# Value sets moved ahead of forget sets, first forget loads and the pairs' operations given rank, in a hybrid HGRN2 and attention block

## The chip, the core and the metric

The kernel runs on one core of a Trainium2 chip. The metric is the time of one execution on the device in microseconds, as the median of several runs; lower is better. The core has five engines that take instructions in order, each from its own queue: TensorE (PE) multiplies matrices, VectorE (DVE) and ScalarE (ACT) work on elements, GpSimd (POOL) here mostly issues transfers, and SyncE (SP) issues the loads of the weights. Engines wait for each other through semaphores.

## The reference

One transformer block over 256 tokens and 256 context tokens of width 2048. All projections come from one matrix, `xn @ w_in`; two branches, a sliding-window attention and a bidirectional gated linear recurrence (HGRN2) of 16 heads of 128, are gated, projected and merged. The part around the change:

```python
xn = rmsnorm(h, norm_gain[l]) * (1.0 + scale) + shift      # cn likewise from ctx
aq, ak, av, ag, hq, hff, hfb, hi, hg, ma, mb = split_columns(xn @ w_in[l])
...
g_f, k_f = hgrn_forget(hff, lb_f_all[l])     # log f and 1-f, f = lb + (1-lb)*sigmoid(z)
g_b, k_b = hgrn_forget(hfb, lb_b_all[l])     # the same for the context: cg_*, ck_*
v_h = to_heads(hi); q_h = to_heads(jax.nn.silu(hq))
s_f = hgrn2_final_state(ck_f, cv_h, cg_f)    # start states from the context
s_b = hgrn2_final_state(flip_t(ck_b), flip_t(cv_h), flip_t(cg_b))
o, _, _ = hgrn2_bidir(q_h, v_h, k_f, g_f, k_b, g_b, s_f, s_b)
hg_branch = hgrn_readout(o, hgrn_norm_gain[l], hg)
```

All of it is float32. The kernel gets that precision from a reduced format by splitting each operand into a high and a low part and multiplying high by high, low by high and high by low.

## The kernel before

**Weights.** A weight tile of 512 KB is loaded by SP's queue into one of four buffers (`raw`). ScalarE copies its high part (`wh`, L76 in general chunks, L605 in the dense phase), VectorE subtracts to get the low part (`wl`, L77, L606); each has three buffers. A chunk of products then runs on TensorE: L91, L92 and L94, or L145 and L148 for the query projections.

**Stages.** After normalisation comes the *dense phase*. It makes the first value projection, one output gate, then 13 column sets and 3 value sets. A column set, `quad_col(d, n)`, computes the forgets F of direction d for two heads with seven sums of products instead of eight (L630 and L633, the operand T or `raw` combined on VectorE, L586; results joined in L623, L624 and L649). Partial sums of a set stand in a tile `s15`, which uses the buffer of the tag `F1` (there is one). F itself uses one of the two buffers of the tag `F0`, and POOL stores it to a DRAM tensor (L655). A value set, `quad_tok`, does the same for values (L702, L704, L707; joined by VectorE in L664); its two result tiles `vo` use both `F0` buffers and POOL stores them (L712).

**Pair stage.** Then eight pairs of heads are worked one after another. `load_forgets(n)` loads F of both directions for pair n back from DRAM into an `F0` and an `F1` buffer (L1089, on POOL's queue, F1 first in the code) and `ctx_decay` runs over the context half: two scans per direction on VectorE (L759 forward, L763 backward; the trace calls them TENSOR_TENSOR_SCAN, the lists of instructions below SCALAR_TENSOR_TENSOR) and one product per direction (L764, into the context half of F). Then the four query chunks are projected and `pair` does the rest: transposes of the context half (`tw`, L904), `grow` (L882, L883, L887, L888) with copies on ScalarE (L814, L817), score blocks `al` (L841), their masking (L856 on VectorE, L853 on ScalarE), `kt` (L947), the state (L967), the outputs `ob` (L979 to L981) and the readout (L991). L783, L788 to L792 prepare its operands, L156 joins the halves of the query projections. `pair` is a generator: it gives up control between its parts, and `weave` puts projections for other parts of the block between them, as many columns as the pair asked for, so that TensorE has work while VectorE and ScalarE do the pair's. Every three such steps a gate chunk of `w_ada` is loaded and summed on VectorE (L196).

**What sets the order.** In both stages TensorE's order is the order of the code. The other engines are ordered ahead of time by a list scheduler: of the instructions that are ready by its own model, the one with the highest priority is next, which is by default the one written first. `tc.high_priority(n)` raises what is written inside it by n. Chunks have `PRIO` (100000), the joining of the sets 2 * `PRIO`, the pairs and `ctx_decay` nothing. Once put in order, an engine's instructions are run in that order, whatever arrives first. A buffer is handed on when the last reader of its former tile is done.

Of the kernel before, what the change touches and what calls it, by code (L numbers as in the profile page):

```python
# [21 lines left out]
PRIO = 100000  # L22

C_Q, C_K, C_V, C_G = 0, 2048, 2560, 3072
C_HQ, C_FF, C_FB, C_HI, C_HG = 5120, 7168, 9216, 11264, 13312
# [13 lines left out]
def block_kernel(ctx: ExitStack, tc: tile.TileContext, x, c, cx, c_ctx, w_ada, b_ada, norm_gain, w_in,  # L39
# [59 lines left out]
    def proj_tok_g(w, col0, src, toks):  # L99


        banks = [bank() for _ in toks]
        for k0 in range(0, KT, 2):
            h, lo = wchunk(w, k0 * P, 2, col0, 512)
            mm_high_first([(banks[i], src(k0 + j, t), (h[:, j, :], lo[:, j, :]), k0 + j == 0, k0 + j == KT - 1)
                           for j in range(2) for i, t in enumerate(toks)])
            yield len(toks) * 6 * 512
        return banks
# [9 lines left out]
    def proj_tok(*a):  # L118
        return result(proj_tok_g(*a))
# [100 lines left out]
    v_dr = [[dram.tile([P, 1024], F32, name=f"v{g}_{t}") for t in range(2)] for g in range(4)]  # L220
# [285 lines left out]
    def run(g):  # L506
        for _ in g:
            pass

    def output_gate(g):  # L510
        bg = yield from proj_tok_g(w_in, C_HG + 512 * g, x_st, range(2))
        for t in range(2):
            sg = base.tile([P, 512], F32, tag="sm", name="sgg", bufs=3)
            act.activation(sg, bg[t], AF.Sigmoid)
            dve.tensor_tensor(sg, bg[t], sg, op=ALU.mult)
            nc.gpsimd.dma_start(hg_dr[g][:, t * 512: (t + 1) * 512], sg)
# [17 lines left out]
    with pl("sp", reuse_waits="tile") as sp:  # L534
# [179 lines left out]
        with tc.manual_schedule(engines={mybir.EngineType.PE}):  # L714
            bv0 = proj_tok(w_in, C_HI, x_st, range(4))
            for g in range(2):
                token_sums(g)
            for t in range(2):
                vo = fp.tile([P, 2, 512], F32, tag="F0", name="vo", bufs=2)
                with tc.high_priority(2 * PRIO):  # L720
                    act.activation(vo[:, 0, :], bv0[t], AF.Copy)
                    dve.tensor_copy(vo[:, 1, :], bv0[2 + t])
                nc.gpsimd.dma_start(v_dr[0][t], vo.rearrange("p a c -> p (a c)"))
            run(output_gate(0))
            for n in range(1, 8):
                for d in range(2):
                    if (d, n) != (0, 1):
                        quad_col(d, 2 * n)
            for g in range(1, 4):
                quad_tok(C_HI + 512 * g, v_dr[g])  # L730

    biases = {}

# [16 lines left out]
    def ctx_decay(F):  # L750


        rev = lambda a: bass.AP(a.tensor, a.offset + T - 2, [list(a.ap[0]), [-1, T - 1]])
        for d in range(2):
            e = base.tile([P, 512], F32, tag="sm", name="e", bufs=3).rearrange("p (h t) -> p h t", h=2)
            for i in range(2):
                if d == 0:
                    pool.memset(e[:, i, T - 1: T], 1.0)
                    dve.tensor_tensor_scan(rev(e[:, i, 0: T - 1]), rev(F[0][:, i, T + 1: 512]), zeros[:, : T - 1], 1.0,  # L759
                                           ALU.mult, ALU.add)  # L760
                else:
                    pool.memset(e[:, i, 0:1], 1.0)
                    dve.tensor_tensor_scan(e[:, i, 1:T], F[1][:, i, T: 511], zeros[:, : T - 1], 1.0, ALU.mult, ALU.add)  # L763
            dve.scalar_tensor_tensor(F[d][:, :, T:], F[d][:, :, T:], -1.0, e, op0=ALU.add, op1=ALU.mult)  # L764
# [248 lines left out]
    def weave(g, filler):  # L1013

        ahead = 0
        for want in g:
            ahead -= want * STEP
            while ahead < 0:
                got = next(filler, None)
                if got is None:  # L1020
                    break
                ahead += got
        run(filler)
# [62 lines left out]
    def load_forgets(n):  # L1086
        F = [fp.tile([P, 2, 512], F32, tag=f"F{d}", name=f"F{d}", bufs=2 - d) for d in range(2)]
        for d in (1, 0):
            nc.gpsimd.dma_start(F[d].rearrange("p i t -> p (i t)"), F_dr[d][n])  # L1089
        ctx_decay(F)  # L1090
        return F
# [48 lines left out]
    with tc.manual_schedule(engines={mybir.EngineType.PE}):  # L1140
        accT = fp.tile([P, 2, 512], F32, tag="acc", name="acc")
        gate, count = gates(), [0]
        grps = [[None] * 3 for _ in range(4)]
        res = [load_forgets(0), None]
        res[1] = result(proj_col_x_g(w_in, C_HQ))
        for n in range(8):
            if n % 2 == 0:
                load_values(n // 2, grps[n // 2])
                load_gate(n // 2, grps[n // 2])
            nxt = [None] * 2  # L1150
            weave(pair(n // 2, n % 2, grps[n // 2], *res), with_gates(inputs(n, nxt)))
            res = nxt
        for f in done:
            f()
# [334 lines left out]
```

## Time and profile before

| | |
|---|---|
| runs | 1617.05, 1620.55, 1621.6 us; median 1620.55 |
| the profiled execution | 1618.51 us, of which the span is 1616.7 us |
| granted TensorE clock, mean over the span | 0.993 |
| TensorE busy | 1581.5 us (98%) |
| VectorE busy | 1153.2 us (71%) |
| ScalarE busy | 863.5 us (53%) |
| moved by DMA | 312.76 MB, mean 193 GB/s |

A row of the page's groups reads: line, engine, operation, output from input, count, then total busy time and mean nanoseconds of one, then the engine's idle time before such instructions and what ended most of it. A row of the waits view names the engine and line that waited, what it waited for, and then total microseconds, times, and the longest. In a timeline row stand start, duration and instruction, and in brackets how long the engine had been idle before it and what released it. In a row of windows stand the stretch and its length, busy time and count for PE, PEld, DVE, ACT and POOL, then the granted clock, the DMA engines' busy share and GB/s.

### The profile page before, as it was taken

The page shows a single profiled execution, that of the slowest core. Times are in us where ns is not written, and L with a number is a line of the kernel's source. Part 1 is how long each engine was busy: PE and PEld are TensorE (multiplying, and loading weights), DVE is VectorE, ACT ScalarE, POOL GpSimd, SP SyncE. Part 2 cuts the span into 40 slices and gives each one's busy share as a digit, 9 for nine tenths or more (in the row PEclk, how much of TensorE's full clock was granted, in tenths as well). Part 3 has the DMA queues.
Part 4 walks back from the last instruction along what each step waited for, and adds up shares of the span by engine and source line. Part 5 has one row for each costly group of instructions (what it writes and reads, how often), then busy time and mean ns, then how long its engine had stood idle before and what let it go on. Part 6 is the DMA issues. An engine that isn't in the chain of part 4 may idle for free. (4 is left out here: it accounts for less than half of the span.)

```text
span 1616.7 us, 26661 instructions
## 1 busy us (share of the span) xinstructions
PE 1581.5 (98%) x10522; PEld 1337.2 (83%) x10522; DVE 1153.2 (71%) x1703; ACT 863.5 (53%) x1337; POOL 84.0 (5%) x183
## 2 busy tenths in 40 slices
PE   7999999999999989999999999999999999999997
PEld 4567888888899978888888888878888888888887
DVE  4449688888877767885887887556567767756664
ACT  4334456656543345664666566434457677744442
POOL 2000000000000010111111010000000000000000
PEclk9999999999999999999999999999999999999999
DMA  9994444444444466664777776567554445467662
GB/s 365 386 371 168 156 131 130 134 142 142 134 141 131 131 241 209 196 222 144 233 242 231 225 237 204 163 213 244 181 183 144 144 138 166 159 230 242 198 208 80
DMA packets 230013, 312.76 MB, mean 193 GB/s; under 512 B 10080, under 2 KB 145664, under 8 KB 228992
## 3 DMA queue, kind: packets, MB, share of 16 engines
q1 hardware_dynamic: 216800, 266.85, 50.5%
q0 software_dynamic: 12368, 43.11, 7.7%
q8 instruction: 82, 1.34, 0.3%
q10 hardware_dynamic: 720, 1.11, 0.2%
q14 instruction: 43, 0.35, 0.1%
HBM read 290.05 MB, written 20.98 MB: 192 GB/s over the span
## 5 line engine op out<-in xcount | busy, mean ns | idle before, releaser
L77 DVE TENSOR_TENSOR wl<-raw,wh 128x1024 fp32r<-128x1024 f32 x308 | 374.6, 1221 | 184.0 <-ACT wh L76 166.6
L76 ACT ACTIVATE wh<-raw 128x1024 fp32r<-128x1024 f32 x308 | 324.8, 1059 | 311.9 <-PE pj L92 189.2
L91 PE MATMUL pj<-wh,xHL 128*128 128x512 f32 (+1 forms) x832 | 326.1, 393 | 2.4 <-DVE hsum L156 1.7
L92 PE MATMUL pj<-wh,xHL 128*128 128x512 f32 (+1 forms) x832 | 320.7, 387 | 0.0
L94 PE MATMUL pj<-wl,xHL 128*128 128x512 f32 (+1 forms) x832 | 215.3, 386 | 0.0
L91 PEld LDWEIGHTS pj<-wh,xHL 128*128 128x128 f32 x832 | 157.0, 189 | 35.2 <-DVE hsum L156 2.6
L92 PEld LDWEIGHTS pj<-wh,xHL 128*128 128x128 f32 x832 | 157.1, 189 | 29.7
L94 PEld LDWEIGHTS pj<-wl,xHL 128*128 128x128 f32 x832 | 154.5, 188 | 32.1 <-DVE wl L77 0.5
L145 PE MATMUL pj<-xHL,wh 128*128 128x512 f32 x512 | 130.8, 397 | 0.0
L605 ACT ACTIVATE wh<-raw 128x1024 fp32r<-128x1024 f32 x76 | 80.4, 1058 | 74.3 <-PE pj L630 22.1
L606 DVE TENSOR_TENSOR wl<-raw,wh 128x1024 fp32r<-128x1024 f32 x76 | 92.8, 1221 | 33.0 <-ACT wh L605 32.9
L145 PEld LDWEIGHTS pj<-xHL,wh 128*128 128x128 f32 x512 | 92.6, 188 | 17.3
L91 PE MATMUL pj<-wh,bH 128*128 128x512 f32 x256 | 101.7, 398 | 3.4 <-ACT wh L76 2.7
L605 ACT ACTIVATE wh<-T 128x1024 fp32r<-128x1024 f32 x57 | 60.5, 1061 | 80.4 <-PE pm L630 19.4
L92 PE MATMUL pj<-wh,bL 128*128 128x512 f32 x256 | 100.8, 395 | 0.1
L606 DVE TENSOR_TENSOR wl<-T,wh 128x1024 fp32r<-128x1024 f32 x57 | 69.6, 1220 | 19.8 <-ACT wh L605 19.6
L148 PEld LDWEIGHTS pj<-xHL,wl 128*128 128x128 f32 x512 | 69.8, 190 | 5.2
L94 PE MATMUL pj<-wl,bH 128*128 128x512 f32 x256 | 71.4, 395 | 0.1
L148 PE MATMUL pj<-xHL,wl 128*128 128x256 f32 x512 | 71.3, 282 | 0.0
L196 DVE SCALAR_TENSOR_TENSOR acc<-raw,cg,acc 128x512 f32<-128x512 f32 x60 | 44.9, 748 | 31.6 <-DMA raw<-in_w_ada_dram 31.1
L887 DVE TENSOR_TENSOR A<-A,X 128x512 f32<-128x512 f32 x96 | 61.9, 685 | 4.5 <-ACT F L814 2.8
L91 PEld LDWEIGHTS pj<-wh,bH 128*128 128x128 f32 x256 | 48.8, 191 | 14.8 <-ACT wh L76 3.6
(356 smaller groups left out, 2763.2 us busy)
## 6 DMA issues: line engine op xcount, KB each, us to landing
raw<-in_w_in_dram SPq DMA_DIRECT2D x300, 512.0 KB, 3.8
raw<-in_w_ada_dram SPq DMA_DIRECT2D x96, 512.0 KB, 7.8
raw<-in_w_o_hgrn_dram SPq DMA_DIRECT2D x32, 512.0 KB, 4.7
raw<-in_w_o_attn_dram SPq DMA_DIRECT2D x32, 512.0 KB, 3.9
F<-F POOLq DMA_DIRECT2D x29, 512.0 KB, 4.8
raw<-in_w_out_dram SPq DMA_DIRECT2D x28, 512.0 KB, 4.3
v<-vo POOLq DMA_DIRECT2D x8, 512.0 KB, 4.0
X<-in_x_dram SPq DMA_DIRECT2D x2, 1024.0 KB, 6.7
```

Source lines behind the costliest of these rows:

```text
L76: act.activation(h[:, :n], raw[:, :n], AF.Copy)
L77: dve.tensor_tensor(lo[:, :n], raw[:, :n], h[:, :n].bitcast(F32), op=ALU.subtract)
L91: pe.matmul(o, s[0], m[0], start=first, stop=False)
L92: pe.matmul(o, s[1], m[0], start=False, stop=False)
L94: pe.matmul(o, s[0], m[1], start=False, stop=last)
L145: pe.matmul(o.rearrange("p (a t) -> p a t", a=2), h[:, j, cs_], xHL[:, :, k0 + j, :T], start=k0 + j == 0, stop=False)
L148: pe.matmul(o[:, :T], lo[:, j, cs_], xH[:, k0 + j, :T], start=False, stop=k0 + j == KT - 1)
L196: dve.scalar_tensor_tensor(acc, wr[:, j, :], cc, acc, op0=ALU.mult, op1=ALU.add)
L605: act.activation(h, src, AF.Copy)
L606: dve.tensor_tensor(lo, src, h.bitcast(F32), op=ALU.subtract)
L887: dve.tensor_tensor(av, av, f.unsqueeze(3).to_broadcast([P, 2, n2, b]), op=ALU.mult)
```

## The change

The change has three parts. In the dense phase the three value sets are written ahead of the 13 column sets instead of behind them. `weave` runs every part of a pair inside `tc.high_priority(2 * PRIO)`, so that on the engines that the scheduler orders a pair's operations outrank the chunks' high and low parts. And the first `load_forgets(0)`, with its `ctx_decay`, is written inside `tc.high_priority(2 * PRIO)`. No instruction is added or removed, and TensorE's order in the pair stage is as before. Lines behind the edits are numbered 4 or 5 higher.

```diff
             run(output_gate(0))
+            for g in range(1, 4):
+                quad_tok(C_HI + 512 * g, v_dr[g])
             for n in range(1, 8):
                 for d in range(2):
                     if (d, n) != (0, 1):
                         quad_col(d, 2 * n)
-            for g in range(1, 4):
-                quad_tok(C_HI + 512 * g, v_dr[g])
...
     def weave(g, filler):

         ahead = 0
-        for want in g:
+        while True:
+            with tc.high_priority(2 * PRIO):
+                want = next(g, None)
+            if want is None:
+                break
             ahead -= want * STEP
...
         gate, count = gates(), [0]
         grps = [[None] * 3 for _ in range(4)]
-        res = [load_forgets(0), None]
+        with tc.high_priority(2 * PRIO):
+            res = [load_forgets(0), None]
         res[1] = result(proj_col_x_g(w_in, C_HQ))
```

POOL's queue at the change from the dense phase to the pair stage, before. `vo` are value tiles, F0_5330 is the first pair's forward forgets (its backward ones, F1_5331, were loaded further up the queue), F0_5746 the second pair's:

```order
L1036 DMA vc_5437<-v0_0_105 128x512
L1036 DMA v_5436<-v0_0_105 128x512
L1036 DMA vc_5437<-v0_1_106 128x512
L1036 DMA v_5436<-v0_1_106 128x512
L1040 DMA gate_5442<-hg0_113 128x1024
L762 MEMSET e_5340 128x1 x2
L712 DMA v3_0_111<-vo_4876 128x1024
L712 DMA v3_1_112<-vo_4877 128x1024
L1089 DMA F0_5330<-F0_0_89 128x1024
L1089 DMA F0_5746<-F0_1_90 128x1024
```

And now. F0_5135 is the forgets tile of the last column set but one, F0_5312 of the last:

```order
L655 DMA F0_7_96<-F0_5135 128x1024
L739 DMA bb_6199<-in_b_merge_dram 128x512
L1040 DMA vc_5437<-v0_0_105 128x512
L1040 DMA v_5436<-v0_0_105 128x512
L1040 DMA vc_5437<-v0_1_106 128x512
L1040 DMA v_5436<-v0_1_106 128x512
L1044 DMA gate_5442<-hg0_113 128x1024
L1093 DMA F0_5330<-F0_0_89 128x1024
L758 MEMSET e_5334 128x1 x2
L762 MEMSET e_5340 128x1 x2
L1093 DMA F1_5331<-F1_0_97 128x1024
L655 DMA F1_7_104<-F0_5312 128x1024
```

The load of F0_5330 has moved from behind the last value stores to behind the store of a column set that is one set old; the load of F1_5331, ahead of the value stores before, now comes after it.

VectorE at the same place, up to the first pair's operands, before. wl_5483 and higher are low parts of the chunks behind the first pair's transposes, e_5334 and e_5340 the scans of F0_5330 and F1_5331 (that of F1_5331 ran further up, between the last value sums):

```order
L77 TENSOR_TENSOR wl_5483<-raw_5480,wh_5482 128x1024
L77 TENSOR_TENSOR wl_5501<-raw_5498,wh_5500 128x1024
L77 TENSOR_TENSOR wl_5519<-raw_5516,wh_5518 128x1024
L156 TENSOR_TENSOR hsum_5450<-pj_5346,hsum_5450 128x256
L156 TENSOR_TENSOR hsum_5455<-pj_5347,hsum_5455 128x256
L759 SCALAR_TENSOR_TENSOR e_5334<-F0_5330,zero_5325 128x255 x2
L792 TENSOR_TENSOR qk_5446<-A_5444 128x512
L789 TENSOR_TENSOR qk_5446<-qk_5446,hsum_5450 128x256
L789 TENSOR_TENSOR qk_5446<-qk_5446,hsum_5455 128x256
L764 SCALAR_TENSOR_TENSOR F0_5330<-F0_5330,e_5334 128x2x256
```

And now, where wl_5417 is the low part of the last query chunk:

```order
L77 TENSOR_TENSOR wl_5417<-raw_5414,wh_5416 128x1024
L759 SCALAR_TENSOR_TENSOR e_5334<-F0_5330,zero_5325 128x255 x2
L77 TENSOR_TENSOR wl_5483<-raw_5480,wh_5482 128x1024
L764 SCALAR_TENSOR_TENSOR F0_5330<-F0_5330,e_5334 128x2x256
L763 SCALAR_TENSOR_TENSOR e_5340<-F1_5331,zero_5325 128x255 x2
L77 TENSOR_TENSOR wl_5501<-raw_5498,wh_5500 128x1024
L792 TENSOR_TENSOR qk_5446<-A_5444 128x512
L764 SCALAR_TENSOR_TENSOR F1_5331<-F1_5331,e_5340 128x2x256
L77 TENSOR_TENSOR wl_5519<-raw_5516,wh_5518 128x1024
L156 TENSOR_TENSOR hsum_5450<-pj_5346,hsum_5450 128x256
```

Both directions' scans and products now stand ahead of the sums of the query projections, F0's behind the last query chunk's low part and F1's behind F0's.

VectorE in the seventh pair (pair 6, counted from 0), as one piece of the difference. F_9595 is the next pair's backward forgets, X_9266 the seventh pair's working tile:

```order
 L856 COPY_PREDICATED X_9266<-mk,al 128x4x32 x3
+L763 SCALAR_TENSOR_TENSOR e<-F_9595,zero 128x255 x2
 L887 TENSOR_TENSOR A<-A,X_9266 128x64x8 x2
-L77 TENSOR_TENSOR wl<-raw,wh 128x1024
-L763 SCALAR_TENSOR_TENSOR e<-F_9595,zero 128x255 x2
+L764 SCALAR_TENSOR_TENSOR F_9595<-F_9595,e 128x2x256
+L77 TENSOR_TENSOR wl<-raw,wh 128x1024
 L887 TENSOR_TENSOR A<-A,X_9266 128x32x16 x2
-L764 SCALAR_TENSOR_TENSOR F_9595<-F_9595,e 128x2x256
```

The scan of F_9595 has moved ahead of an L887 and of a low part, both of which were ahead of it.

## The prediction

> **What bounds the kernel now.** I read the page's head first, then TensorE's waits.
>
> ```profile
> span 1616.7 us, 26661 instructions
> ...
> PE 1581.5 (98%) x10522; PEld 1337.2 (83%) x10522; DVE 1153.2 (71%) x1703; ACT 863.5 (53%) x1337; POOL 84.0 (5%) x183
> ...
> L77 DVE TENSOR_TENSOR wl<-raw,wh 128x1024 fp32r<-128x1024 f32 x308 | 374.6, 1221 | 184.0 <-ACT wh L76 166.6
> L76 ACT ACTIVATE wh<-raw 128x1024 fp32r<-128x1024 f32 x308 | 324.8, 1059 | 311.9 <-PE pj L92 189.2
> ```
>
> ```profile
> PE tw L904 <- DVE F L764: 5.2, 1, 5.2
> PE ob L981 <- DVE X L967: 3.6, 3, 2.3
> PE pj L91 <- ACT wh L76: 2.7, 1, 2.7
> ...
> PE pj L91 <- DVE hsum L156: 1.7, 2, 1.4
> ```
>
> TensorE is busy for 98% of the span, so time can come only from its waits and from a slow clock; VectorE's and ScalarE's idle time is waiting for TensorE. The one wait of size that touches this change is the 5.2 us of the first pair's transposes (tw) for VectorE's F. I followed it back through the timelines of POOL, ScalarE, VectorE and TensorE:
>
> ```profile
> 576.39 0.54 POOL L712 DMA_DIRECT2D v<-vo  x1 [1.59 <-DVE vo L664]
> 582.13 0.53 POOL L1089 DMA_DIRECT2D F<-F  x1 [5.21 <-DMA v<-vo]
> ```
>
> ```profile
> 588.00 0.63 ACT L783 ACTIVATE A<-F 128x512 f32<-128x512 f32 x1 [0.78 <-DMA F<-F]
> ```
>
> ```profile
> 575.40 0.69 DVE L664 TENSOR_TENSOR vo<-pj,sn 128x512 f32<-128x512 f32 x1 [0.31 <-PE pj L707]
> ...
> 588.52 1.26 DVE L759 TENSOR_TENSOR_SCAN e<-F,zero 128x255 f32<-128x255 f32 x2
> 589.70 0.67 DVE L792 TENSOR_TENSOR qk<-A 128x512 f32<-128x512 f32 x1
> ...
> 590.95 0.68 DVE L764 SCALAR_TENSOR_TENSOR F<-F,e 128x512 f32<-128x512 f32 x1
> ```
>
> ```profile
> 580.79 2.00 PE L145 MATMUL pj<-xHL,wh 128*128 128x512 f32 x8
> ...
> 583.58 2.00 PE L145 MATMUL pj<-xHL,wh 128*128 128x512 f32 x8
> 585.42 1.11 PE L148 MATMUL pj<-xHL,wl 128*128 128x256 f32 x8
> 591.69 1.97 PE L904 MATMUL tw<-cs,F 128*128 128x128 f32 x8 [5.16 <-DVE F L764]
> ...
> 598.04 0.40 PE L91 MATMUL pj<-wh,xHL 128*128 128x512 f32 x1
> ...
> 600.80 0.39 PE L91 MATMUL pj<-wh,xHL 128*128 128x512 f32 x1
> ```
>
> The last value tile is finished at 576.1, its store holds the F0 buffer until 582.13, the forget load into that buffer lands at 588.00 (5.87 us after its issue), scan and product take until 591.6. The four query chunks (2.79 us each, 580.79 to 583.58) ended at 586.53. After the wait TensorE is slow:
>
> ```profile
> 586.60:591.70 5.10, 0.01 (x1) 0.01 (x1) 4.99 (x10) 1.86 (x6) 0.25 (x4) 0.89 0.98 382
> 591.70:598.04 6.34, 6.34 (x20) 5.34 (x21) 5.40 (x11) 3.70 (x7) 0.00 (x0) 0.55 0.11 28
> 648.69:652.58 3.89, 3.89 (x20) 3.89 (x21) 2.77 (x6) 0.75 (x2) 0.00 (x0) 0.58 0.90 292
> 704.61:706.94 2.33, 2.33 (x20) 2.33 (x21) 2.33 (x4) 1.40 (x3) 0.00 (x0) 1.00 0.89 299
> ```
>
> ```profile
> 706.94 1.04 PE L904 MATMUL tw<-cs,F 128*128 128x128 f32 x8
> 707.74 0.48 PE L91 MATMUL pj<-wh,xHL 128*128 128x512 f32 x1
> ```
>
> The third number from the end is the granted clock. At 0.55, transposes and one chunk took 6.35 us (591.69 to 598.04). At full clock the transposes take 0.80 (706.94 to 707.74) and a chunk 2.76 (598.04 to 600.80), 3.56 together. So the place costs 5.16 + 2.79 = 7.95 us.
>
> [...]
>
> **The change, part by part.** *Value sets first.* No instruction is added or removed; three sets of products move ahead of 13. Crossing from column to value products now costs nothing, and I cost the two new crossings at nothing on this row, in which such a crossing lies and TensorE is busy for 40.00 of 40:
>
> ```profile
> 440.00:480.00 40.00, 40.00 (x299) 38.32 (x298) 30.03 (x30) 19.46 (x23) 1.19 (x3) 1.00 0.45 146
> ```
>
> If the cover went, a late high part costs what the only such wait does, 2.7 us (waits, third row). The queue's weight loads are permuted with their products; none is added.
>
> *First forgets with high rank.* POOL's rows (in the section on the change) show the F0 load now behind stores issued one column set earlier, and the F1 load behind the last column set's s15 tile, which lies in F1's only buffer. I put t = 0 at the end of the sixth product of that last set. When s15 comes free is read from an earlier set:
>
> ```profile
> 451.45 2.00 PE L630 MATMUL pm<-xHL,wh 128*128 128x512 f32 x8
> ```
>
> ```profile
> 453.98 0.42 DVE L624 TENSOR_TENSOR sg<-s 128x256 f32<-128x256 f32 x1
> ```
>
> The sixth product ended at 451.45 and the last read at 454.40, so s15 is free at t = 2.95. With 5.87 us of load, F1 lands at 8.8; F0, issued near t = 0, lands near 6. TensorE still has the seventh product (2.8) and four query chunks (11.2), and wants F0 at 14.0 and F1 at 14.4. VectorE's new order is scan F0, a chunk's low part, product F0, scan F1, a low part, L792, product F1. The second low part needs the buffer of the third query chunk, whose high matmuls end at 8.4 + 2.0 = 10.4; plus 1.06 of ScalarE and 1.22 is 12.7; plus L792 and the product, 0.6 and 0.7, is 14.0. So F1 is ready 0.4 us early, F0 three. Landing by 10.6 would still do, a load of 7.6 us. I take 0.2 us left for misfits: gain 7.95 - 0.2 = 7.75. Bounds: 5.16 without the clock's part, 7.95 with nothing left.
>
> *Pairs above chunks.* Most waits of the pairs are not a matter of rank. In pair 0 a gate product stands in VectorE's order between mask copies and waits for its weights:
>
> ```profile
> 640.68 0.75 DVE L196 SCALAR_TENSOR_TENSOR acc<-raw,cg,acc 128x512 f32<-128x512 f32 x1 [3.47 <-DMA raw<-in_w_ada_dram]
> ```
>
> That stretch of VectorE's order is unchanged, so the 2.27 us wait behind it, and its slow clock (3.89 against 2.33 in the windows rows, 1.56), stay. Two small waits have changed rows:
>
> ```profile
> 881.80 0.49 PE L981 MATMUL ob<-X,A 128*128 128x128 f32 x2 [0.92 <-DVE X L967]
> ```
>
> ```profile
> 997.03 0.51 PE L91 MATMUL pj<-wh,xHL 128*128 128x512 f32 x1 [0.32 <-DVE hsum L156]
> ```
>
> At 997.03 both hsum rows now precede the gate product: -0.3. In pair 4 a gate product has moved behind two sums: -0.5 (between 0 and -0.9, the middle). Against them stands pair 6, where the next pair's F1 scan moved ahead of an L887 and a low part:
>
> ```profile
> 963.60 0.54 POOL L1089 DMA_DIRECT2D F<-F  x1 [6.96 <-PE al L841]
> ```
>
> ```profile
> DMA to landing us min/median/max: 3.6/6.1/8.5
> ```
>
> ```profile
> 965.74 0.97 DVE L856 COPY_PREDICATED X<-mk,al 128x128 f32<-128x128 uint8 x3
> 967.04 1.29 DVE L887 TENSOR_TENSOR A<-A,X 128x512 f32<-128x512 f32 x2 [0.33 <-ACT Kmt L817]
> ...
> 969.69 1.27 DVE L763 TENSOR_TENSOR_SCAN e<-F,zero 128x255 f32<-128x255 f32 x2 [0.22 <-DMA F<-F]
> ```
>
> ```profile
> 981.83 0.66 PE L947 MATMUL kt<-cs,A 128*128 128x128 f32 x4
> ```
>
> The scan already waits for its load, until 969.69. Reached at 966.7, it holds VectorE for 3 us, with L887 and a low part queued behind. Replaying the new order from there: scan to 971.0, L887 972.2, product 972.8, low part 974.0, L887 975.2, two low parts 977.5, gate product 978.2, L887 979.4, gate product and low part 981.3, L887 982.5. kt wants it at 981.83: +0.7. A load of 3.6 us makes it 0, one of 8.5 us +3.1.
>
> **Sum.** -7.75 - 0.3 - 0.5 + 0.7 = -7.85 against the profiled execution's 1618.51 us (1.8 around the span): 1610.7. The median of the runs, 1620.55, lies 2.04 above that execution, so I predict 1612.7 on the median's footing. About 0.3%, 4.9 us, separates a change from none: below 1615.7 is faster, above 1625.4 slower.
>
> **The rivals.** *Pair waits close too.* If ranks pull pair work forward enough, the waits of pair 0 (2.27 + 1.56) and before pair 2 (1.4) go, and pair 6 costs nothing: 1612.7 - 5.9 = 1606.8. For it: these waits end on VectorE. Against: the gate weights that hold it are not ranked.
>
> *F1 late.* The chain moves from the value store to s15. If the F1 load takes 10 us among the prefetches (DMA share 0.98 while TensorE waits, first windows row), tw waits 2.4 and some 1.6 of slow clock follow: 1612.7 + 4.0 - 0.2 = 1616.5. Against: the longest such load took 8.5, costing 0.9 and a little clock, 1614.5.
>
> *The time is not passed on.* If the freed 8 us turn into waits for weights later, it ends near 1618 to 1622. Against: TensorE waits for a high part once in the trace.
>
> *Slower: scans and pair rows block the chunks.* Place: every pair, VectorE's in-order queue, low parts behind a scan that waits for its load, as in pair 6. Price 0.7 us each by the median load, 3.1 by the longest. To pass 1625.4 it must cost 12.7 us above my sum, 1.6 in each of eight pairs; at 2.5 each (20 us less the 0.7 counted) it gives about 1632. Against: only pair 6 shows a scan moved ahead of its landing, and low parts have three buffers, two chunks' time.
>
> **Chances.** My forecast (1609.5 to 1615.6) 0.65; pair waits close too 0.10; F1 late 0.09, mostly just inside "same"; not passed on 0.08; slower 0.08. Faster is the first two, 0.75; same the next two, 0.17; slower 0.08. The range 1606 to 1619 leaves out the slower case, most of "not passed on" and the best of the second.
>
> **What would show it.** Right: the first tw waits under 1 us for L764, the granted clock there is 1.00, F1's load is issued about 11 us before tw; the 2.27 us ob wait and its 0.58 clock remain; the scan in pair 6 waits about 3 us and kt under 1. Wrong: tw still waits over 2 us, new TensorE waits for L76 or L77 in the pairs, or waits at the crossings of the dense phase.

## The result, and the profile after

| | before | after |
|---|---|---|
| median of the runs compared | 1619.96 us (6 runs, 1617.05 to 1621.6) | 1615.03 us (6 runs, 1613.12 to 1616.71) |
| ratio | | 0.9972, interval 0.9959 to 0.9985 |
| profiled execution, and its span | 1618.51, 1616.7 us | 1614.37, 1612.6 us |
| granted clock | 0.993 | 0.996 |

The change saves 4.5 us (2.4 to 6.6), where 7.85 was forecast. The sign is clear; the size is about the 0.3% that the prediction set as the least change. The head of the page of the changed kernel, then TensorE's waits in it (microseconds in total, times, the longest):

```profile
span 1612.6 us, 26672 instructions
...
PE 1579.2 (98%) x10522; PEld 1336.6 (83%) x10522; DVE 1152.4 (71%) x1703; ACT 863.7 (54%) x1337; POOL 84.8 (5%) x183
```

```profile
PE ob L981 <- DVE X L967: 5.8, 3, 3.2
...
PE kt L947 <- DVE A L887: 0.9, 2, 0.7
...
PE al L962 <- ACT X L853: 0.8, 1, 0.8
PE pj L91 <- DVE hsum L156: 0.8, 1, 0.8
...
PE tw L904 <- DVE F L764: 0.5, 1, 0.5
```

The wait of 5.2 us for F is down to 0.5. In its place stand 2.2 us more for X in front of `ob`, a new `al` wait of 0.8, and 0.4 more for `kt`; behind the pairs, waits for high parts grew from 2.7 to 3.5. The timeline of the changed kernel at the first pair, POOL, VectorE and TensorE in turn:

```profile
570.73 0.55 POOL L1040 DMA_DIRECT2D vc<-v  x1 [9.00 <-DMA raw<-in_w_in_dram]
...
572.84 0.53 POOL L1044 DMA_DIRECT2D gate<-hg  x1
573.37 0.53 POOL L1093 DMA_DIRECT2D F<-F  x1
...
575.72 0.53 POOL L1093 DMA_DIRECT2D F<-F  x1 [0.80 <-DVE sg L624]
...
581.58 1.27 DVE L759 TENSOR_TENSOR_SCAN e<-F,zero 128x255 f32<-128x255 f32 x2 [1.11 <-DMA F<-F]
...
584.48 1.26 DVE L763 TENSOR_TENSOR_SCAN e<-F,zero 128x255 f32<-128x255 f32 x2
...
587.38 0.69 DVE L764 SCALAR_TENSOR_TENSOR F<-F,e 128x512 f32<-128x512 f32 x1
...
586.06 1.11 PE L148 MATMUL pj<-xHL,wl 128*128 128x256 f32 x8
587.01 0.60 PE L904 MATMUL tw<-cs,F 128*128 128x128 f32 x4
588.12 0.66 PE L904 MATMUL tw<-cs,F 128*128 128x128 f32 x4 [0.51 <-DVE F L764]
...
591.37 0.39 PE L91 MATMUL pj<-wh,xHL 128*128 128x512 f32 x1
```

Five loads of the first group's values and gate (issued from 570.73 to 572.84) stand ahead of the F0 load on POOL's queue. It is issued at 573.37, and the scan waits for it until 581.58: 8.2 us. F1's load is issued at 575.72, and its scan at 584.48 does not wait. TensorE stops for 0.51 us between the transposes of the two directions, and the clock stays up:

```profile
586.60:591.70 5.10, 4.59 (x27) 3.81 (x27) 4.91 (x10) 4.09 (x8) 0.78 (x5) 1.00 0.90 296
643.25:647.16 3.91, 3.91 (x20) 3.91 (x21) 2.77 (x6) 0.75 (x2) 0.00 (x0) 0.57 0.94 323
984.67:987.83 3.16, 0.00 (x1) 0.00 (x1) 3.16 (x7) 1.60 (x3) 0.00 (x0) 1.00 0.54 180
987.83:991.79 3.96, 3.96 (x20) 3.96 (x21) 2.00 (x4) 0.75 (x2) 0.00 (x0) 0.57 0.90 304
572.00:582.00 10.00, 10.00 (x61) 8.88 (x60) 5.90 (x9) 7.28 (x10) 3.23 (x10) 1.00 0.96 353
```

The two rows at 643 and 988 are the stretches behind the `ob` waits of pairs 0 and 6, both at 0.57. The last row is the time of the F0 load: DMA engines busy for 96%, 353 GB/s.

**Where the time went.** I cut both spans at the start of the last query chunk's low products (the L148 row with xHL, wl ahead of the first `tw`: 585.42 before, 586.06 after), and then at the first `tw` row of each pair.

| stretch | before | after | difference |
|---|---|---|---|
| up to the last query chunk | 585.42 | 586.06 | +0.64 |
| from there through the first chunk behind `tw` | 12.62 | 5.31 | -7.31 |
| rest of pair 0 | 54.54 | 55.79 | +1.25 |
| pairs 1, 2, 3 | 54.36, 67.40, 54.55 | 54.09, 66.74, 55.77 | +0.29 |
| pairs 4, 5 | 55.25, 55.58 | 54.09, 54.31 | -2.43 |
| pair 6 | 54.56 | 59.63 | +5.07 |
| pair 7 and all behind | 622.42 | 620.81 | -1.61 |
| span | 1616.7 | 1612.6 | -4.1 |

The place of the change gave 7.31, and pair 6 took 5.07 back. The timelines of pair 6 show how: first POOL, VectorE, SP and TensorE of the changed kernel, then VectorE and SP of the kernel before.

```profile
956.03 0.54 POOL L1093 DMA_DIRECT2D F<-F  x1 [6.58 <-PE al L841]
...
961.59 1.27 DVE L763 TENSOR_TENSOR_SCAN e<-F,zero 128x255 f32<-128x255 f32 x2 [2.24 <-DMA F<-F]
...
975.49 2.35 DVE L77 TENSOR_TENSOR wl<-raw,wh 128x1024 fp32r<-128x1024 f32 x2
...
983.19 1.54 DVE L196 SCALAR_TENSOR_TENSOR acc<-raw,cg,acc 128x512 f32<-128x512 f32 x2 [4.80 <-DMA raw<-in_w_ada_dram]
984.64 2.35 DVE L77 TENSOR_TENSOR wl<-raw,wh 128x1024 fp32r<-128x1024 f32 x2
986.92 1.12 DVE L967 SCALAR_TENSOR_TENSOR X<-so,X,al 128x128 f32<-128x128 f32 x4
...
976.73 0.37 SPq L66 DMA_DIRECT2D raw<-in_w_ada_dram  x1
...
974.28 0.66 PE L947 MATMUL kt<-cs,A 128*128 128x128 f32 x4
...
987.83 0.74 PE L981 MATMUL ob<-X,A 128*128 128x128 f32 x2 [3.16 <-DVE X L967]
```

```profile
981.00 2.35 DVE L77 TENSOR_TENSOR wl<-raw,wh 128x1024 fp32r<-128x1024 f32 x2
...
987.29 1.54 DVE L196 SCALAR_TENSOR_TENSOR acc<-raw,cg,acc 128x512 f32<-128x512 f32 x2 [3.40 <-DMA raw<-in_w_ada_dram]
...
982.24 0.37 SPq L66 DMA_DIRECT2D raw<-in_w_ada_dram  x1
```

Count from the pair's first `tw` (932.16 after, 939.72 before). The scan waits 2.24 us for its load, as forecast (about 3). The low parts behind it, among them the pair that starts at 975.49, are late: 43.33 after, 41.28 before. In both kernels a gate's weight load goes out just as the first of these two low parts ends and frees its `raw` buffer (976.7 and 982.2), so it is issued at 44.57 instead of 42.52. It then takes 6.46 us to the gate sum (976.73 to 983.19) instead of 5.05. The sum, two low parts and L967 follow in VectorE's order, and `ob` waits 3.16 us for L967, where the kernel before waited for nothing. So 2.05 us came from the later issue and 1.41 from a slower load. The slow clock behind the wait adds 1.6: the 3.96 us from 987.83 to the next `tw` take 2.34 at full clock (993.79 to 996.13 with part 2 alone, below). `kt`, where the prediction looked, does not wait.

### The profile page after: what moved, and what is told of

Its sections match the earlier page's. It is cut to its first block, busy times and chain, and to the rows that moved or that the text cites. A ratio compares the mean times of both kernels' runs of the same rounds, so it can differ in the third digit from the quotient of the medians.

```text
span 1612.6 us, 26672 instructions
## 1 busy us (share of the span) xinstructions
PE 1579.2 (98%) x10522; PEld 1336.6 (83%) x10522; DVE 1152.4 (71%) x1703; ACT 863.7 (54%) x1337; POOL 84.8 (5%) x183
## 3 DMA queue, kind: packets, MB, share of 16 engines
q10 hardware_dynamic: 720, 1.11, 0.2%
## 5 line engine op out<-in xcount | busy, mean ns | idle before, releaser
L148 PEld LDWEIGHTS pj<-xHL,wl 128*128 128x128 f32 x512 | 69.8, 190 | 5.1
L148 PE MATMUL pj<-xHL,wl 128*128 128x256 f32 x512 | 71.3, 282 | 0.0
L887 DVE TENSOR_TENSOR A<-A,X 128x512 f32<-128x512 f32 x96 | 61.9, 687 | 4.2 <-ACT F L814 2.8
```

Of the source, the lines that this page charges most:

```text
L148: pe.matmul(o[:, :T], lo[:, j, cs_], xH[:, k0 + j, :T], start=False, stop=k0 + j == KT - 1)
L887: dve.tensor_tensor(av, av, f.unsqueeze(3).to_broadcast([P, 2, n2, b]), op=ALU.mult)
```

## The experiments

In each, the diff is against the changed kernel unless it says otherwise. Ratios are against the kernel before, on the same chip. The lengths below are of one profiled execution each; their spread without any cause is seen in the third experiment.

**The three parts, one at a time.** Part 1 alone (the value sets):

```diff
-        while True:
-            with tc.high_priority(2 * PRIO):
-                want = next(g, None)
-            if want is None:
-                break
+        for want in g:
...
-        with tc.high_priority(2 * PRIO):
-            res = [load_forgets(0), None]
+        res = [load_forgets(0), None]
```

> Only the first part of the change: value sets ahead of column sets, no rank for the pairs, none for the first forgets. Theory A (the value sets' place closes the first pair's gap by itself, and the pairs' rank is what costs 5.1 us in pair 6 while giving back about 3.1 in pairs 2, 4 and 5 and costing 1.2 in pair 3): tw waits under 1 us, tw to tw over pair 6 is about 54.6 us as before the change, and the time is 1615 - 3.2 = 1611.8. Rival B (the loss in pair 6 comes from the earlier start of the pair stage against the gate weights' loads, whatever the rank): pair 6 takes 59.6 us here too, 1615 or more. Rival C (the rank of the first forgets is needed to bring their loads forward): tw waits 4 to 5 us, about 1620.

Measured 1615.54 us, ratio 0.9970 (0.9958 to 0.9983): all of the change's gain, but not the 1611.8 that theory A expected. Its first pair:

```profile
582.13 1.27 DVE L759 TENSOR_TENSOR_SCAN e<-F,zero 128x255 f32<-128x255 f32 x2 [2.30 <-DMA F<-F]
...
588.68 0.66 PE L904 MATMUL tw<-cs,F 128*128 128x128 f32 x4 [1.70 <-DVE F L764]
```

The F0 load, issued at 572.73, took 9.4 us, and `tw` still waits 1.70, not under 1. Pair 6, without rank, took 56.74 us from `tw` to `tw`, between the two theories; with rank it took 59.63.

Part 2 alone (the pairs' rank):

```diff
             run(output_gate(0))
-            for g in range(1, 4):
-                quad_tok(C_HI + 512 * g, v_dr[g])
             for n in range(1, 8):
...
+            for g in range(1, 4):
+                quad_tok(C_HI + 512 * g, v_dr[g])
...
-        with tc.high_priority(2 * PRIO):
-            res = [load_forgets(0), None]
+        res = [load_forgets(0), None]
```

> Only the second part: the pairs rank above the chunks, the sets in their old order. Theory A: tw waits 5.2 us as before, tw to tw over pair 6 is about 59.6 us with a wait of about 3 us at ob, and the time is about 1620 + 3.2 = 1623. Rival B: pair 6 takes 54.6 us, and the ranks' small gains give about 1618.

Measured 1619.86 us, ratio 0.9999 (0.9990 to 1.0009): nothing, where theory A expected 1623. The `tw` wait stays, at 5.87. Pair 6 took 59.32 us, as theory A said, with 2.54 of wait in front of `ob` and, ahead of that, a new one of 1.11 for a low part that stands behind the scan in VectorE's order:

```profile
972.23 1.19 PE L94 MATMUL pj<-wl,xHL 128*128 128x512 f32 x4 [1.11 <-DVE wl L77]
...
993.79 0.49 PE L981 MATMUL ob<-X,A 128*128 128x128 f32 x2 [2.54 <-DVE X L967]
```

Part 3 alone (the first forgets' rank): the value sets as in part 2's diff, the loop over `g` as in part 1's.

> Only the third part: the first forgets with rank, nothing else. Every engine's order of instructions is then the same as before the change, so all theories expect the time before, ratio 1.000, and a first tw wait of 5.2 us. It also shows how far the waits behind gate weights differ between two executions of one order: if pair 6's 54.6 us before the change was a fast gate load (5.0 us, against 6.5 to 7.0 in the value-sets-first kernels), pair 6 takes 55.5 to 57 us here with an ob wait of 1 to 2 us; if the value sets' place made it slower, it takes 54.6 again.

Measured 1619.13 us, ratio 1.0005 (0.9994 to 1.0016). This part does nothing: with it alone every engine's list is row for row that of the kernel before, and added to part 1 it changes no row either. So the profile of this kernel shows how far two executions of one order differ. Pair 6 took 55.28 (54.56 before), pair 3 took 55.81 with a `kt` wait of 0.80 (54.55 before). The `ob` wait of pair 0 was 2.29, but this time without a slow clock behind it:

```profile
647.71:650.04 2.33, 2.33 (x20) 2.33 (x21) 2.18 (x5) 0.62 (x2) 0.00 (x0) 1.00 0.90 322
```

**Pair 6.** The rank is withheld from that pair alone:

```diff
-    def weave(g, filler):
+    def weave(g, filler, rank):
...
-            with tc.high_priority(2 * PRIO):
+            with tc.high_priority(rank):
...
-            weave(pair(n // 2, n % 2, grps[n // 2], *res), with_gates(inputs(n, nxt)))
+            weave(pair(n // 2, n % 2, grps[n // 2], *res), with_gates(inputs(n, nxt)), 2 * PRIO if n in (0, 1, 2, 3, 4, 5, 7) else 0)
```

> The changed kernel with the rank left off in pair 6 alone, where the next pair's scan then stands behind a low part as before the change; the ranks of the other pairs stay. Theory A: pair 6 takes about 54.6 us instead of 59.6, the other pairs as in the changed kernel, 1615 - 5 = 1610. Rival B: pair 6 stays near 59.6 us and the time near 1615. Rival D (the two sums of the merge that the rank groups ahead of the low parts, not the scan, are late for ob): the ob wait in pair 6 falls only by some 0.7 us, 1614.

Measured 1614.99 us, ratio 0.9959 (0.9943 to 0.9976). Pair 6 took 56.33 us, 3.3 less than in the changed kernel (5 were expected), its `ob` wait 1.55 at full clock. The total, expected at 1610, does not resolve it: the interval overlaps the changed kernel's, and the profiled execution lost 2.0 us in pair 0 (63.14 from the last query chunk instead of 61.10, with an `al` wait of 1.74). Over all kernels whose gate chunks stand in pair 6 as in before, its length parts by rank without overlap: 54.56, 55.28, 56.33 and 56.74 without; 57.33, 59.32 and 59.63 with (the 57.33 is of a kernel further down).

The issue of the gate's weight load, again counted from the pair's first `tw`, shows the cause more plainly. It goes out at 44.57, 44.61 and 46.57 us in the three kernels with rank and at 42.52, 42.78, 42.84 and 43.32 in the four without. The scan's wait for its load is 2.24, 2.25 and 3.98 in the first three and 0.22, 0.47, 0.53 and 0.83 in the others, so in all seven the issue comes at 42.3 to 42.6 us plus that wait. The time from the issue to the gate sum does not part by rank: 6.46, 5.73 and 5.77 with it, 5.05, 6.99, 5.47 and 6.04 without. So the later issue is the rank's doing, and the 1.41 us of slower load are not.

Behind pair 6 the rank gives a part back: the wait for hsum at the start of pair 7, 0.32 to 1.36 us in the four kernels without it, is gone. From the first `tw` of pair 6 to the end of the span the two groups overlap, 677.0 to 678.6 us without and 677.1 to 680.4 with, so what the rank of pair 6 costs the whole is not resolved.

The other hold on pair 6 is the gate chunk itself. Here pairs 6 and 7 get none; it moves behind the pairs:

```diff
+            side_n = inputs(n, nxt)
-            weave(pair(n // 2, n % 2, grps[n // 2], *res), with_gates(inputs(n, nxt)))
+            weave(pair(n // 2, n % 2, grps[n // 2], *res), side_n if n in (6, 7) else with_gates(side_n))
```

> The changed kernel without gate chunks during pairs 6 and 7, so that neither pair 6's chunk nor one of pair 7's can stand ahead of pair 6's state products; they are made behind the pairs, at a cost there of 10 us or more that does not matter for the question. Theory A (the gate weights arrive last): no ob wait over 0.5 us in pair 6, tw to tw 54.5 to 55.5 us. Rival (pair 6's own chain, behind the forget scan, is late): ob waits 2 to 3 us again, 58 to 60 us.

One execution: 1632.17 us. Pair 6 took 55.42 us with its rank kept, as short as without rank, although the scan waits 2.65 us there: the rank costs there only together with the gate sum ahead of L967. Of the `ob` wait 1.06 us is left, which has another cause: two low parts ahead of L967 wait 5.02 us for high parts.

```profile
983.89 2.36 DVE L77 TENSOR_TENSOR wl<-raw,wh 128x1024 fp32r<-128x1024 f32 x2 [5.02 <-ACT wh L76]
986.17 1.12 DVE L967 SCALAR_TENSOR_TENSOR X<-so,X,al 128x128 f32<-128x128 f32 x4
```

The whole became slower behind the pairs: 640.99 us from the last `tw` to the end, against 620.81.

**Gate chunks in pair 0.** In the changed kernel pair 0 still waits at `al` and `ob`. Its SP, VectorE and TensorE:

```profile
628.52 0.37 SPq L66 DMA_DIRECT2D raw<-in_w_ada_dram  x1
...
635.25 0.75 DVE L196 SCALAR_TENSOR_TENSOR acc<-raw,cg,acc 128x512 f32<-128x512 f32 x1 [4.21 <-DMA raw<-in_w_ada_dram]
635.92 0.29 DVE L856 COPY_PREDICATED X<-mk,al 128x128 f32<-128x128 uint8 x1
...
636.58 1.16 PE L962 MATMUL al<-v,Kmt 128*128 128x128 f32 x8 [0.80 <-ACT X L853]
...
643.25 0.80 PE L981 MATMUL ob<-X,A 128*128 128x128 f32 x2 [2.27 <-DVE X L967]
```

The gate's weights took 6.73 us from issue to sum; before it was 6.00 (issued at 634.68, summed at 640.68). The last mask copy stands behind the sum, and `al` waits for what follows it. Part 1 alone, with no gate chunk in pair 0 (the diff is against part 1 alone):

```diff
+            side_n = inputs(n, nxt)
-            weave(pair(n // 2, n % 2, grps[n // 2], *res), with_gates(inputs(n, nxt)))
+            weave(pair(n // 2, n % 2, grps[n // 2], *res), side_n if n in (0,) else with_gates(side_n))
```

> Value sets first without any rank, and no gate chunk (a load of w_ada and its sums on VectorE) during pair 0; they are made later instead. If pair 0's waits at own and ob hang on the gate weights that stand between the mask copies in VectorE's order, both go with the slow clock behind them, and pair 0 takes 2.3 + 1.6 + 0.8 = 4.7 us less than with value sets first alone; the total falls by that less what the displaced chunks cost later, so by 2 to 5 us. If they hang on the pair's own work, pair 0 stays and the total too.

Measured 1612.04 us, ratio 0.9955 (0.9939 to 0.9971); the interval overlaps that of part 1 alone. From the last query chunk pair 0 took 56.69 us, against 62.08 with part 1 alone: 5.4 less. Pair 1 took 59.34 against 55.97: 3.4 more, since all later chunks move up and one now stands ahead of L967 in pair 1, where `ob` waits:

```profile
697.60 0.49 PE L981 MATMUL ob<-X,A 128*128 128x128 f32 x2 [2.25 <-DVE X L967]
```

So the gate chunk holds pair 0, and moving it moves the wait. Taking the chunks of both pairs 0 and 6 out, in the changed kernel and with part 1 alone, was meant to close both (the diff is as above, with `n in (0, 6)`):

> The changed kernel (value sets first, pairs ranked), without gate chunks during pairs 0 and 6; they are made later, in the stage behind the pairs. Theory A (in those two pairs the weights of a gate chunk, which stands ahead of the state's products in VectorE's order, arrive last, and every wait at own and ob follows from it): pair 0 takes about 55.5 us instead of 60.2, pair 6 about 55 instead of 59.6, no ob wait over 0.5 us in either, and 1615 falls by 9 less what the displaced chunks cost in other pairs (3.4 us in pair 1 when pair 0's were displaced alone), so 1607 to 1611. Rival (the pair's own chain is the limit there and the gate chunk only happens to stand in it): pairs 0 and 6 stay within 1 us of 60.2 and 59.6, 1614 to 1616.

> The same displacement of gate chunks, with value sets first but the pairs unranked. If the ranks help once the gate chunks of pairs 0 and 6 are out of the way (they advance sums and products of the pairs), this is 1 to 2 us slower than the ranked version; if the ranks move nothing that TensorE waits for, the two agree within 1 us.

Measured 1635.34 us, ratio 1.0094 (1.0078 to 1.0111), and 1637.47, ratio 1.0109 (1.0091 to 1.0127): 15 and 17 us slower than before, where the first was expected at 1607 to 1611. The kernel without rank is the slower one by 2 us, as expected if the ranks help there, but the intervals overlap. Pair 0 became short in both (56.70 and 56.56 us from the last query chunk), pair 6 did not. In the first of them the chunks of pairs 1 and 5 now stand ahead of L967 (58.48 and 57.60 us), two sums of the next pair's chunk stand ahead of pair 6's L967 (58.71), and behind the last `tw` it took 640.44 us against 620.81; in the second 643.37. What happens there, in the first kernel, by SP, VectorE, ScalarE and TensorE:

```profile
1072.62 1.94 SPq L66 DMA_DIRECT2D raw<-in_w_o_hgrn_dram  x2
...
1070.72 0.69 DVE L204 TENSOR_REDUCE redg<-tqg 128x4 f32<-128x512 f32 x1 [3.33 <-PE tqg L202]
...
1071.84 4.69 DVE L196 SCALAR_TENSOR_TENSOR acc<-raw,cg,acc 128x512 f32<-128x512 f32 x6
...
1076.36 1.06 ACT L76 ACTIVATE wh<-raw 128x1024 fp32r<-128x1024 f32 x1 [10.26 <-DMA raw<-in_w_o_hgrn_dram]
...
1077.47 0.80 PE L91 MATMUL pj<-wh,bH 128*128 128x512 f32 x1 [6.79 <-ACT wh L76]
```

VectorE waits 3.33 us for a gate's transposes with six gate sums behind. The next weights of the output projection are issued 0.78 us after the first of these sums started, that is, when it has freed a `raw` buffer, and TensorE waits 6.79 us. Gate chunks that the pairs no longer take hold the weight buffers here.

The last try leaves the rank and lets the gate chunks in only up to the third part of each pair, at a shorter interval, to keep them away from L967:

```diff
+            phase[0] += 1
             ahead -= want * STEP
...
-            count[0] += got
-            if count[0] >= 3 * STEP:
-                count[0] -= 3 * STEP
+            if phase[0] <= 3:
+                count[0] += got
+            if count[0] >= 1.75 * STEP:
+                count[0] -= 1.75 * STEP
...
+            phase[0] = 0
```

> The changed kernel with gate chunks counted only during the first three parts of each pair, at a shorter interval, and the rest made behind the pairs. By theory A the ob waits shrink where the chunk now stands behind the state's products in VectorE's order (pairs 0, 2, 3) and stay where it stands ahead of them (pairs 4, 5 and 6): pair 0 about 55.5 us, pair 6 57 to 60, total 1608 to 1612. If gate weights do not matter, 1614 to 1616.

Measured 1646.06 us, ratio 1.0156 (1.0137 to 1.0176), where 1608 to 1612 was expected. Pair 0 took 56.48 us from the last query chunk, but pairs 4 and 6 took 63.80 and 61.47, with `ob` waits of 5.02 and 5.61 (in pair 4 a gate sum waits 7.78 us for its weights two low parts ahead of L967), and it took 642.14 behind the last `tw`. Keeping one pair free of gate chunks cost nothing there (619.35 without pair 0's); the three ways to keep more away cost about 20 us and more.

**The F0 load.** If it takes 8 to 9 us because of the loads ahead of it, fewer of them must shorten it. This kernel leaves out two of the three: the first group's `v` and its gate are not loaded but set to zero, 1.0 MB of the 1.5 that stand ahead of F0.

```diff
-            for z in (1, 0):
+            for z in ((1, 0) if g else (1,)):
                 nc.gpsimd.dma_start(grp[z][:, t, :], dv[:, z, :])
+        if g == 0:
+            pool.memset(grp[0], 0.0)
...
+        if g == 0:
+            pool.memset(grp[2], 0.0)
+            return
         nc.gpsimd.dma_start(grp[2].rearrange("p t c -> p (t c)"), hg_dr[g])
```

> The changed kernel with two of the three loads of the first value group that stand ahead of the first forget load on POOL's queue left out (v and the output gate, 1 MB, set to zero instead, so the first two pairs' results are not those of the reference). If the forget loads are slow there (8.2 to 9.4 us from issue to landing, 5.9 before the change) because these 1 MB and the weight loads share the DMA engines, F0's load takes 5 to 6.5 us, and the first tw does not wait. If the load is slow for another reason, it takes over 8 us and tw waits 0.5 to 1.7 us.

One execution: 1607.68 us. Timeline (POOL, VectorE, TensorE) and window:

```profile
573.14 0.54 POOL L1098 DMA_DIRECT2D F<-F  x1
...
578.60 1.27 DVE L759 TENSOR_TENSOR_SCAN e<-F,zero 128x255 f32<-128x255 f32 x2
...
586.57 1.04 PE L904 MATMUL tw<-cs,F 128*128 128x128 f32 x8
```

```profile
572.00:582.00 10.00, 10.00 (x60) 8.84 (x59) 6.97 (x11) 6.97 (x10) 2.49 (x8) 1.00 0.88 304
```

The scan starts 5.46 us after the issue without waiting, so the load took that or less, and `tw` does not wait. The load was issued within 0.3 us of the changed kernel's (573.37) and landed 3 us earlier, so the loads left out made it slow there.

**Put together.** The changed kernel with no gate chunk in pair 0 and no rank in pair 6 (the two diffs above):

> Candidate for a faster version: value sets first, ranks in all pairs but pair 6, no gate chunks in pair 0. From the two single edits (1612.0 without pair 0's chunks and without ranks, 1615.0 without pair 6's rank) theory A expects pair 0 at 55.7 us, a pair 1 of 58 to 59, pair 6 at 55 to 56, and 1610 to 1613; 1615 or more if the displaced chunks take back what pair 0 gives.

Measured 1611.86 us, ratio 0.9957 (0.9942 to 0.9972). Pair 0 took 55.68 us from the last query chunk, pair 6 55.36; pairs 1 and 5 took 56.43 and 57.76, with the displaced chunks. The total is level with that of part 1 without the chunk.

The same, with the loads of the first group's `v` and gate behind the forgets and nothing left out: POOL copies two columns of F1 into each tile ahead of its load, so the load waits for F1.

```diff
+        if g == 0:
+            pool.tensor_copy(grp[0][:, :, 0:1], res[0][1][:, :, 0:1])
+            for t in range(2):
+                nc.gpsimd.dma_start(grp[0][:, t, :], v_dr[0][t].rearrange("p (a c) -> p a c", a=2)[:, 0, :])
...
+        if g == 0:
+            pool.tensor_copy(grp[2][:, :, 0:1], res[0][1][:, :, 0:1])
```

> The last candidate (value sets first, no rank in pair 6, no gate chunks in pair 0) with the first group's v and output gate loaded behind the first forgets: a one-column copy from the landed F1 tile makes their loads wait for it. Nothing is left out. If the 1 MB ahead of the forget loads is what makes them slow, F0's load takes 5 to 6.5 us instead of 8 to 9.4 and the first tw does not wait; v and gate are first read 45 us later and hide. About 1 us less than the version without it, 1610 to 1611.5. If the forgets of the second pair are now late (their store stands behind the copies on POOL's queue), pair 0 or the start of pair 1 takes more, and the gain is lost.

Measured 1610.71 us (1607.92 to 1612.25), ratio 0.9938 (0.9922 to 0.9953): 10 us (7.6 to 12.6) faster than before, and its interval lies below the changed kernel's (0.9959 to 0.9985). Against the kernel just above (0.9942 to 0.9972) the intervals still overlap. Timeline:

```profile
571.49 0.53 POOL L1099 DMA_DIRECT2D F<-F  x1
...
578.73 1.27 DVE L759 TENSOR_TENSOR_SCAN e<-F,zero 128x255 f32<-128x255 f32 x2 [3.61 <-DMA F<-F]
...
586.71 1.04 PE L904 MATMUL tw<-cs,F 128*128 128x128 f32 x8
```

F0 lands at 578.73 instead of 581.58. Its load took 7.2 us, not the 5 to 6.5 expected: it is issued 1.65 us earlier than with the two loads left out, directly behind the two that remain, and lands at the same time. `tw` has no wait, and pair 0 takes 54.63 us from the last query chunk (before: 67.16).

## Why the prediction was right or wrong

**The first pair: right, a little too high.** F1's load was issued 11.3 us ahead of `tw` (575.72 to 587.01), `tw` waited 0.51, the clock was 1.00. The place gave 7.31 where the term said 7.75. Two steps were mis-sized. One is the length of the F0 load: 5.87 was taken from the row before, 8.2 was measured. The other is F0's deadline. The 7.6 us that the replay allowed are for F1's load, which took 7.8 and landed at 583.51, 0.97 ahead of its scan; for F0 the replay saw 3 us to spare. But F1's scan and product stand behind F0's in VectorE's order, and from F0's scan to the end of F1's product it took 6.5 us (581.58 to 588.07). So F0's load had to land 0.5 us earlier, after 7.7 us; F0, not F1, was late. Before, the five loads of the first group went out between 569.90 and 572.02, 10 us ahead of F0's; now they go out directly ahead of it. The order in the section on the change has those five rows, and I priced the load without them. That they are the cause is shown by the kernel with 1.0 MB less ahead (5.46 or less, no wait); in the last one, also with 1.0 MB less, the load took 7.24 from an earlier issue, and `tw` does not wait either. That the dense phase came out 0.64 longer is no sign of the new crossings: the last query chunk's low products start between 584.82 and 586.86 us in the 14 profiles, with the value sets first or last.

**Which part does it: wrong.** The prediction put the new place of the F loads under the first forgets' rank. Part 1 alone closes most of the gap (1.70 of wait is left) and part 3 alone changes no row.

**Pair 0: half right.** The 2.27 us `ob` wait stayed, with its slow clock (0.57), because gate weights hold VectorE, as said. That these weights would come 0.73 us later in their turn (6.73 instead of 6.00 from issue), giving `al` a wait of 0.80, was not in the sum; rest of pair 0: +1.25.

**Pairs 4 and behind.** The 0.92 wait of pair 4 is gone (-1.16 in that pair, forecast -0.5), and so is that for hsum at 997 (0.3). Pair 5's -1.27 and the wait for hsum of pair 2 (1.39 to 0.75) were not forecast. Pairs 4 and 5 part by rank in all kernels with the gate chunks where they were: pair 4 takes 54.1 to 54.8 us with rank and 55.2 to 55.3 without, pair 5 54.1 to 54.7 and 55.1 to 55.6. So the ranks do it, but by which rows in pair 5 I did not follow. Pair 3's +1.22 has its `kt` wait in the kernel with the old order too (0.80), so I take no cause for it.

**Pair 6: the step that failed.** Forecast +0.7 at `kt`; measured +5.07, with no wait at `kt`. The scan was late by about what was said (2.24), but my replay stopped at the next matmul that VectorE feeds. The low parts behind the scan also free the weight buffers, and the gate weights issued from them end in a sum ahead of L967. What the rank costs in that pair is between 0.6 and 4.8 us: 59.32 (part 2 alone) against 54.56 and 55.28 in the old order, 59.63 and 57.33 against 56.74 (part 1 alone) and 56.33 (no rank in 6). The 5.07 is at the upper end by chance: pair 6 of this execution of before is the shortest of all kernels' here, with the fastest gate load of the seven above, and in the changed kernel the `ob` wait happened to be followed by a slow clock (1.6 us), while those of 2.54 and 2.42 us in the other two ranked kernels were not. The value sets' place may add to it: of the four kernels without rank, the two with the value sets first took 1 to 2 us longer there. By one execution each that is not shown.

**The net of the ranks.** Part 2's ratio of 0.9999 is their sum. In pairs 2 to 5 they save about 1 us (part 2 alone 231.94 against 232.78 before; the changed kernel 230.91 against 232.06 with part 1 alone), and pair 6 takes it back, as far as the lengths of single executions show. The forecast for them, 0.7 - 0.3 - 0.5 = -0.1, came out right in its sum by luck, by terms that were each off.

**The sum.** The profiled execution gained 4.1 us where 7.85 was forecast. Lost against the terms: 0.64 up to the last query chunk, 0.44 at the place, 1.25 in pair 0, 0.29 in pairs 1 to 3, 4.37 in pair 6; won: 1.93 in pairs 4 and 5, 1.31 behind; together 3.75. Most of what is missing is pair 6. That the time still came inside the forecast range is in part luck: the misses in pairs 4 to 6 have opposite signs.

**The rivals.** "Pair waits close too" did not happen. "F1 late" had the right place and the wrong load. "Scans block the chunks" was right in one pair out of eight, at 0.6 to 4.8 us instead of 0.7 to 3.1. Its sign, a TensorE wait for a low part, does not show in the changed kernel, but with part 2 alone (1.11 us in pair 6).

**The clock.** Of the 7.31 us gained at the place 4.65 are wait (5.16 less 0.51); the other 2.66, the slow clock above all (0.55 over 591.70 to 598.04 before, 1.00 over 586.60 to 591.70 after), are near the 2.79 that the prediction took from its rows. What the other runs show of waits and clocks stands in the last section.

## What to carry to other kernels

Price a moved load by what stands ahead of it at its new place, not by its time at the old one (here the F0 load took 5.9 us at the old place, 8.2 at the new one, and at most 5.5 there with 1.0 MB less ahead), and take its deadline from everything that stands behind its reader in that engine's order. When rank lets an operation that waits for a load go first on an in-order engine, follow everything behind it, also to the buffers it frees and to the loads that go into them: here 2.2 us at a scan made a weight load 2.05 us later, which with a slower load on top became 3.2 us of wait at another matmul 26 us after the scan. When time comes free at one place, look which load was just in time there, since it may be what waits next: here, with the wait of 5.2 us gone, `tw` still waited 0.51, for the chain behind the F0 load that took 8.2.

## What the runs showed of the hardware

The granted clock after a wait of TensorE. I took all waits of 1.3 us or more behind 560 us in the 14 profiles, and the granted clock of the 3.9 us that follow each. Of 15 waits from 1.31 to 1.92 us none was followed by a slow clock (all 1.00). Of 35 from 1.96 to 2.79 us, 22 were (0.50 to 0.69), and 13 were not. Of 18 from 3.03 to 6.79 us all were (0.50 to 0.68). Two rows stand above, after waits of 2.27 and 2.29 us at the same place in one order of instructions: 0.58 in the kernel before (648.69, in the prediction), 1.00 in that with part 3 alone (647.71). The first costs 3.89 - 2.33 = 1.6 us more for the same work.

The shortest of the 35, 1.96 us with another wait of 0.62 us ahead of it, had a slow clock behind it (last kernel, 1043.58, clock 0.56). In the order above a wait of 2.3 us costs 1.6 us more in one execution and nothing more in another; what decides between the two is not shown. That may be one source of the 3 to 9 us between the lowest and the highest run of one kernel here; it was not followed run by run.

The first pair's F0 load of 512 KB took 5.9 us from issue to its reader (before), 8.2 (changed), 9.4 (part 1 alone), 7.2 (last kernel), and at most 5.5 with 1.0 MB less ahead. The DMA engines' busy share over 572 to 582 us was 0.96 in the changed kernel and 0.88 in the one with less ahead. The share alone does not set the time: it was no lower (1.04 in the same view, 408 GB/s) over 582.13 to 588.00 before, where F0's load took 5.9 us. In the changed kernel the gate's load, directly ahead of F0's on POOL's queue, landed at 579.77 and F0's at 581.55. Whether the loads ahead hold F0 on the queue or by sharing the engines is not shown.
